# Second SwiGLU: down's pair 1 of k-tiles by seven products of quarters in place of eight

## The chip, the cores and the metric

The kernel runs on one core of a Trainium2 chip. The metric is the device time of one execution, in microseconds (us): the median of several runs, each the time of the slowest core, which here is the only one. Beside the timed runs stands one execution taken by the hardware profiler; its instructions, waits and transfers are what this document calls the profile and the trace. TensorE is called PE, VectorE DVE, ScalarE ACT, GpSimd POOL; SP is the sync engine, which issues most DMAs.

## The reference

Two layers of a transformer trunk on 256 tokens of width 1024, all in fp32. Each layer has a SwiGLU, a mixer (attention) and a second SwiGLU, with an RMSNorm ahead of each:

```python
def rms_norm(x, g):
    xf = x.astype(jnp.float32)
    y = xf * lax.rsqrt(jnp.mean(xf * xf, axis=-1, keepdims=True) + EPS)
    return (y * g.astype(jnp.float32)).astype(x.dtype)

def swiglu(h, w_gate, w_up, w_down):
    return (jax.nn.silu(h @ w_gate) * (h @ w_up)) @ w_down

...
    for layer in range(DEPTH):
        h = rms_norm(x, ffn1_norm[layer])
        x = x + 0.5 * swiglu(h, ffn1_w_gate[layer], ffn1_w_up[layer], ffn1_w_down[layer])
...
        h = rms_norm(x, ffn2_norm[layer])
        x = x + 0.5 * swiglu(h, ffn2_w_gate[layer], ffn2_w_up[layer], ffn2_w_down[layer])
    return rms_norm(x, final_norm)
```

`w_gate` and `w_up` are 1024 x 2816, `w_down` is 2816 x 1024. The change concerns the second of the four SwiGLUs (layer 0, `ffn2`), which the code calls stage 2.

## The kernel before

**Tiles.** The 256 tokens are two token tiles (`tt` 0 and 1) of 128. Every fp32 matrix product is made of parts: a weight tile is split on the core into a high part (`hi`, ACT, line 477) and a low part (`lo`, the rest, DVE, line 480), the activations likewise, and `mm` issues three matmuls for what the document calls one **product**: high by high (line 469), activation high by weight low (470), activation low by weight high (471), each 128x128 by 128x512, into one PSUM bank.

**A SwiGLU.** `ffn` goes through five chunks of 512 columns of gate and up and one of 256; each chunk's gated result (`glu`) goes through `turned_over` (two ACT copies, lines 554 and 558, with a transposing DMA of SP between them, line 556) and `split_psum` (`g_h`, `g_l`), and stays as the left operand of down. Down's 22 k-tiles are taken in 11 pairs, in the order of the table `DOWN`. A pair written `p` is plain: its two weight rows are two splits of 128x1024, and 2 k-tiles x 2 token tiles x 2 column halves make eight products.

**Seven for eight.** A pair written `s` treats the pair's activations (2 token tiles x 2 k-tiles) and weights (2 k-tiles x 2 halves) as two matrices of 2 x 2 blocks and forms the product of these with seven products (`seven`), by sums on both sides, in the manner of Strassen and Winograd. The weight sums are made by `strassen`: after the first split (one block, `b11`) DVE runs three adds (line 395), and the splits that follow are the raw second row of blocks, the two sums in `two`, and the two sums written back over the raw tile:

```python
        splits = [
            Split(second[:, 0:1, :], [1], then=all_sums),
            Split(first, [1]),
            Split(first, [1], kind="sum"),
            Split(second, [1], True, kind="sum"),
        ]
```

The high and low parts of the sums are called `shi` and `slo`; there are three buffers for them, and seven for the plain parts (`FIT`). The activation sums are made when the chunk that holds the pair comes back transposed: `quarters` copies blocks to a tile of that name (ACT, lines 699 and 702) and subtracts (DVE, line 705), `sums_of` runs two more DVE instructions (712, 713) and splits the result into `k..h` (ACT) and `k..l` (DVE). In that case token tile 1 needs one `g_h` and `g_l` block less (384 columns for 512). In the end `combine` adds the four products that are not accumulated in place to x, once for all `s` pairs of the stage. The first `s` pair of a stage also sets the pace at which weights are prepared (`DOWN_RATE`).

The table `SEVEN` does the same with the last k-tiles of some chunks of gate and up: in stage 2 the chunks 1 (three groups of seven products) and 3 (two groups).

**What sets the order.** The order on every engine is the order in which the code issues, with no scheduler behind it. `mm` calls `tick` once per product; `tick` steps the small tasks (silu, glu, transposes, `quarters`), each of which says for how many products it rests, and calls `supply` at a set rate, which issues the next `hi` on ACT and, at the next step, its `lo` on DVE. The raw weights come over SP's queue into three buffers of 1 MB; a new load is issued when the last split of a buffer has been read. An engine works strictly in its order, so an instruction that waits holds up all behind it.

Of the kernel before, what the change touches and what calls it, by code (L numbers as in the profile page):

```python
# [34 lines left out]

DOWN = {
    0: "p0 p1 p2 s3 p4 s5 p6 s7 p8 p10 p9",
    2: "p0 p2 p1 p3 s5 p4 s7 p10 s8 p6 p9",
    3: "p0 p2 s5 s3 p4 s8 p10 p1 s6 p9 p7",
    5: "p3 p0 s2 s5 p4 s1 p9 s7 s8 p6 p10",  # L40
}
# [1525 lines left out]
```

## Time and profile before

| | before |
|---|---|
| timed runs | 944.22 us median of 3 (943.14 to 944.48) |
| profiled execution | 943.06 us, of which the span of instructions is 941.3 us |
| PE busy | 920.8 us (98%) |
| DVE busy | 789.1 us (84%) |
| ACT busy | 679.4 us (72%) |
| mean granted clock of TensorE | 0.998 |

The second SwiGLU begins before 290 us with the plain chunk 0; chunk 1's seven-product groups end near 321 us, down runs from 396 us to about 450 us. Its busy time in some stretches, from the view by windows (busy us with the number of instructions, then the granted clock, the DMA share and GB/s):

```profile
300.00:310.00 10.00, 10.00 (x46) 8.29 (x45) 8.93 (x13) 8.90 (x12) 0.00 (x0) 1.00 0.60 159
310.00:320.00 10.00, 8.01 (x35) 6.13 (x34) 9.93 (x12) 7.74 (x10) 0.00 (x0) 1.00 0.31 105
320.00:330.00 10.00, 10.00 (x45) 8.26 (x44) 8.99 (x11) 6.02 (x7) 0.00 (x0) 1.00 0.89 315
...
400.00:410.00 10.00, 10.00 (x46) 8.29 (x45) 8.17 (x13) 9.17 (x15) 0.00 (x0) 1.00 0.85 270
410.00:420.00 10.00, 10.00 (x45) 8.28 (x45) 9.93 (x13) 6.41 (x9) 0.00 (x0) 1.00 0.54 182
```

The columns after the window are PE, weight loads, DVE, ACT and POOL. A stretch in which PE has 10.00 of 10 is bound by the matmuls; in the one from 310 us PE lacks 2 us while DVE has no pause.

### The profile page before, as it was taken

The page shows a single profiled execution, that of the slowest core. Times are in us where ns is not written, and L with a number is a line of the kernel's source. Part 1 is how long each engine was busy: PE and PEld are TensorE (multiplying, and loading weights), DVE is VectorE, ACT ScalarE, POOL GpSimd, SP SyncE. Part 2 cuts the span into 40 slices and gives each one's busy share as a digit, 9 for nine tenths or more (in the row PEclk, how much of TensorE's full clock was granted, in tenths as well). Part 3 has the DMA queues.
Part 4 walks back from the last instruction along what each step waited for, and adds up shares of the span by engine and source line. Part 5 has one row for each costly group of instructions (what it writes and reads, how often), then busy time and mean ns, then how long its engine had stood idle before and what let it go on. Part 6 is the DMA issues. An engine that isn't in the chain of part 4 may idle for free.

```text
span 941.3 us, 12409 instructions
## 1 busy us (share of the span) xinstructions
PE 920.8 (98%) x4399; PEld 752.5 (80%) x4399; DVE 789.1 (84%) x1228; ACT 679.4 (72%) x1091; POOL 92.6 (10%) x152
## 2 busy tenths in 40 slices
PE   9999999999999999999999999999999999999997
PEld 6887888877778788888888778777878788878886
DVE  6799779778869989788878888999877787988797
ACT  7777875477787777875757778657877577769753
POOL 1300000064410000000100000008030000000001
PEclk9999999999999999999999999999999999999999
DMA  8858865554336677867457777566433458488651
GB/s 297 291 158 255 249 209 216 180 154 99 105 94 199 221 214 235 255 204 265 140 163 236 186 239 223 204 249 172 151 119 135 135 172 253 127 274 254 184 224 45
DMA packets 129343, 183.16 MB, mean 195 GB/s; under 512 B 50688, under 2 KB 63744, under 8 KB 129280
## 3 DMA queue, kind: packets, MB, share of 16 engines
q1 hardware_dynamic: 128704, 181.58, 61.0%
q8 instruction: 34, 0.56, 0.2%
q10 hardware_dynamic: 576, 0.79, 0.2%
q14 instruction: 29, 0.24, 0.1%
HBM read 169.76 MB, written 1.05 MB: 181 GB/s over the span
## 4 chain that ended last, share of the span: by engine, by line
PE 69%; DVE 15%; ACT 7%; DMA 4%; issue 4%; POOL 1%; SPq 0%; POOLq 0%; ACTq 0%; DVEq 0%
PE pj L469 10%; PE pj L470 10%; PE pj L471 9%; PE s L470 9%; PE s L471 9%; PE s L469 9%; DVE lo L480 6%; ACT hi L477 2%; PE o L1039 2%; PE o L470 1%; PE o L471 1%; PE o L469 1%; PE tp L1118 1%; DVE raw L395 1%; DVE two L395 1%
## 5 line engine op out<-in xcount | busy, mean ns | idle before, releaser
L480 DVE TENSOR_TENSOR lo<-raw,hi 128x1024 fp32r<-128x1024 f32 (+1 forms) x372 | 375.9, 1030 | 79.0 <-ACT hi L477 77.2
L477 ACT ACTIVATE hi<-raw 128x1024 fp32r<-128x1024 f32 (+1 forms) x372 | 319.7, 890 | 54.9 <-PE pj L471 14.5
L470 PE MATMUL s<-lo,th 128*128 128x512 f32 x373 | 145.6, 390 | 2.6 <-DVE lo L480 2.6
L469 PE MATMUL pj<-hi,th 128*128 128x512 f32 x367 | 146.6, 400 | 1.3 <-ACT glu L765 1.3
L469 PE MATMUL s<-hi,th 128*128 128x512 f32 x373 | 146.2, 392 | 0.3 <-ACT hi L477 0.3
L471 PE MATMUL s<-hi,tl 128*128 128x512 f32 x373 | 145.3, 390 | 0.0
L470 PE MATMUL pj<-lo,th 128*128 128x512 f32 x367 | 143.5, 391 | 1.7 <-DVE lo L480 1.6
L471 PE MATMUL pj<-hi,tl 128*128 128x512 f32 x367 | 143.2, 390 | 0.0
L470 PEld LDWEIGHTS s<-lo,th 128*128 128x128 f32 x373 | 70.0, 188 | 18.3 <-DVE lo L480 4.2
L469 PEld LDWEIGHTS s<-hi,th 128*128 128x128 f32 x373 | 70.0, 188 | 14.9 <-ACT hi L477 0.6
L470 PEld LDWEIGHTS pj<-lo,th 128*128 128x128 f32 x367 | 69.1, 188 | 16.0 <-DVE lo L480 3.3
L471 PEld LDWEIGHTS s<-hi,tl 128*128 128x128 f32 x373 | 70.0, 188 | 14.4
L469 PEld LDWEIGHTS pj<-hi,th 128*128 128x128 f32 x367 | 69.0, 188 | 15.6 <-ACT glu L765 1.7
L471 PEld LDWEIGHTS pj<-hi,tl 128*128 128x128 f32 x367 | 68.9, 188 | 14.5
L489 POOL TENSOR_TENSOR rstd<-var,mhalf 128x1 f32<-128x1 f32 (+2 forms) x16 | 17.1, 1070 | 594.8 <-DVE var L487 453.4
L558 ACT COPY turned<-glu 128x1024 uint16<-128x1024 uint16 (+1 forms) x48 | 60.1, 1253 | 6.8 <-DMA glu<-turned 6.8
L554 ACT COPY turned<-glu 128x1024 uint16<-128x1024 uint16 (+1 forms) x48 | 46.3, 965 | 14.8 <-DVE glu L792 7.0
L469 PE MATMUL s<-hi,g_h 128*128 128x512 f32 (+1 forms) x131 | 51.4, 392 | 0.0
L471 PE MATMUL s<-hi,g_l 128*128 128x512 f32 (+1 forms) x131 | 50.9, 388 | 0.0
L470 PE MATMUL s<-lo,g_h 128*128 128x512 f32 (+1 forms) x131 | 50.8, 388 | 0.0
L477 ACT ACTIVATE shi<-two 128x1024 fp32r<-128x1024 f32 x30 | 31.7, 1058 | 26.1 <-DVE two L395 25.9
L477 ACT ACTIVATE shi<-raw 128x1024 fp32r<-128x1024 f32 x30 | 31.7, 1056 | 23.5 <-PE s L471 13.0
(483 smaller groups left out, 1681.4 us busy)
## 6 DMA issues: line engine op xcount, KB each, us to landing
raw<-in_ffn_w_down SPq DMA_DIRECT2D x44, 1024.0 KB, 5.2
raw<-in_ffn_w_up SPq DMA_DIRECT2D x28, 1024.0 KB, 5.2
raw<-in_ffn_w_gate SPq DMA_DIRECT2D x26, 1024.0 KB, 5.2
raw<-in_ffn_w_gate SPq DMA_DIRECT2D x35, 512.0 KB, 3.9
raw<-in_ffn_w_up SPq DMA_DIRECT2D x32, 512.0 KB, 5.0
raw<-in_odd_w_qkv SPq DMA_DIRECT2D x12, 1024.0 KB, 5.4
raw<-in_even_w_in SPq DMA_DIRECT2D x4, 1024.0 KB, 5.0
raw<-in_even_w_out SPq DMA_DIRECT2D x8, 512.0 KB, 5.7
```

The costliest lines, as they stand in the source:

```text
L395: add = lambda o, x, y: self.nc.vector.tensor_tensor(o, x, y, op=ALU.add)
L469: mm(ps, h, wh, start=first, stop=False)
L470: mm(ps, h, wl, start=False, stop=False)
L471: mm(ps, l, wh, start=False, stop=last)
L477: self.nc.scalar.activation(hi, src, AF.Copy)
L480: self.nc.vector.tensor_tensor(lo, src, hi.bitcast(F32), op=ALU.subtract)
L489: nc.gpsimd.tensor_tensor(r[:, :n], v[:, :n], self.mhalf[:, :n], op=ALU.pow)
L554: self.nc.scalar.copy(planes.rearrange("p (h c) -> p h c", h=2), back.rearrange("p (c h) -> p h c", h=2))
L558: self.nc.scalar.copy(planes.rearrange("p (c h) -> p h c", h=2), back.rearrange("p (h c) -> p h c", h=2))
L1039: self.nc.tensor.matmul(O[64 * s : 64 * s + 64, i * P : i * P + P], v(b0 + i, s, kc), pT[s][:, i, kc, :], start=(kc == 0), stop=(kc == 1),)
L1118: nc.tensor.transpose(tb[:, o : o + P], p[:, i, kc * P : kc * P + P], self.ident)
```

## The change

One entry of the table of down's pairs: in stage 2, pair 1 (k-tiles 2 and 3, the second pair of down's 22 k-tiles) is `s` instead of `p`. It stays the third pair in the order, and is now the first `s` pair of the stage, so that the tasks that `seven` finishes on its first call, the banks it takes and `DOWN_RATE` come two pairs earlier.

```diff
 DOWN = {
     0: "p0 p1 p2 s3 p4 s5 p6 s7 p8 p10 p9",
-    2: "p0 p2 p1 p3 s5 p4 s7 p10 s8 p6 p9",
+    2: "p0 p2 s1 p3 s5 p4 s7 p10 s8 p6 p9",
     3: "p0 p2 s5 s3 p4 s8 p10 p1 s6 p9 p7",
     5: "p3 p0 s2 s5 p4 s1 p9 s7 s8 p6 p10",
 }
```

Pair 1's activations lie in chunk 0, which comes back transposed while chunk 1 runs. On DVE, in the second and third group of chunk 1, the rows before are these (`turned_3198` is chunk 0's result for token tile 1; `raw_3100` and `raw_3132` are the weights of the second and third group):

```order
L480 TENSOR_TENSOR slo_3252<-two_3229,shi_3251 128x1024
L480 TENSOR_TENSOR g_0_l_3279<-turned_3198,g_0_h_3278 128x512
L480 TENSOR_TENSOR slo_3286<-raw_3100,shi_3285 128x1024
L480 TENSOR_TENSOR lo_3295<-raw_3132,hi_3294 128x512
L395 TENSOR_TENSOR two_3301<-raw_3132 128x1024
L395 TENSOR_TENSOR raw_3132<-two_3301,raw_3132 128x512
L395 TENSOR_TENSOR raw_3132<-raw_3132 128x512
L480 TENSOR_TENSOR lo_3306<-raw_3132,hi_3305 128x1024
```

And now, from the same `slo` on:

```order
L480 TENSOR_TENSOR slo_3254<-two_3229,shi_3253 128x1024
L705 TENSOR_TENSOR quarters_3237<-turned_3198,quarters_3237 128x2x128
L480 TENSOR_TENSOR slo_3289<-raw_3100,shi_3288 128x1024
L480 TENSOR_TENSOR g_0_l_3286<-turned_3198,g_0_h_3285 128x384
L712 TENSOR_TENSOR quarters_3237<-quarters_3237 128x128
L713 TENSOR_TENSOR quarters_3237<-quarters_3237 128x128
L480 TENSOR_TENSOR lo_3301<-raw_3132,hi_3300 128x512
L395 TENSOR_TENSOR two_3307<-raw_3132 128x1024
L395 TENSOR_TENSOR raw_3132<-two_3307,raw_3132 128x512
L395 TENSOR_TENSOR raw_3132<-raw_3132 128x512
L480 TENSOR_TENSOR lo_3312<-raw_3132,hi_3311 128x1024
```

Three instructions are new, and the `g_l` is smaller and stands behind the second `slo`. The last row is the `lo` that PE's first product with the third group's raw row needs. Further on, one `k2l` is new, between the first and the second `lo` of chunk 2.

On ACT, at the same place, before (`turned_3182` is token tile 0):

```order
L558 COPY turned_3182<-glu_3151 128x2x512
L477 ACTIVATE g_0_h_3237<-turned_3182 128x512
L477 ACTIVATE hi_3240<-raw_3100 128x1024
L477 ACTIVATE shi_3251<-two_3229 128x1024
L558 COPY turned_3198<-glu_3192 128x2x512
L477 ACTIVATE g_0_h_3278<-turned_3198 128x512
L477 ACTIVATE shi_3285<-raw_3100 128x1024
```

and now:

```order
L558 COPY turned_3182<-glu_3151 128x2x512
L699 ACTIVATE quarters_3237<-turned_3182 128x256
L477 ACTIVATE g_0_h_3239<-turned_3182 128x512
L477 ACTIVATE hi_3242<-raw_3100 128x1024
L477 ACTIVATE shi_3253<-two_3229 128x1024
L558 COPY turned_3198<-glu_3192 128x2x512
L702 ACTIVATE quarters_3237<-turned_3198 128x128
L477 ACTIVATE g_0_h_3285<-turned_3198 128x384
L477 ACTIVATE shi_3288<-raw_3100 128x1024
```

Two copies are new, both ahead of the `shi` of the second group's last sums. A `k2h` follows later, between the two `shi` of the third group.

The third place is DVE in the first pairs of down. Before (`raw_3853` is pair 2, `raw_3908` pair 1, `raw_3937` pair 3):

```order
L480 TENSOR_TENSOR lo_4000<-raw_3853,hi_3999 128x1024
L480 TENSOR_TENSOR lo_4012<-raw_3908,hi_4011 128x1024
L480 TENSOR_TENSOR lo_4025<-raw_3908,hi_4024 128x1024
L480 TENSOR_TENSOR k14l_4019<-quarters_3914,k14h_4018 128x512
L480 TENSOR_TENSOR lo_4042<-raw_3937,hi_4041 128x1024
```

and now, with pair 2 called `raw_3863`, pair 1 `raw_3918` and pair 3 `raw_3947`:

```order
L480 TENSOR_TENSOR lo_4010<-raw_3863,hi_4009 128x1024
L480 TENSOR_TENSOR lo_4022<-raw_3918,hi_4021 128x512
L395 TENSOR_TENSOR two_4028<-raw_3918 128x1024
L395 TENSOR_TENSOR raw_3918<-two_4028,raw_3918 128x512
L395 TENSOR_TENSOR raw_3918<-raw_3918 128x512
L480 TENSOR_TENSOR lo_4039<-raw_3918,hi_4038 128x1024
L480 TENSOR_TENSOR k14l_4033<-quarters_3924,k14h_4032 128x512
L675 SCALAR_TENSOR_TENSOR glu_4067<-s_3999,rstd_3030,silu_4053 128x256
L480 TENSOR_TENSOR slo_4070<-two_4028,shi_4069 128x1024
L480 TENSOR_TENSOR g_16_l_4064<-turned_3949,g_16_h_4063 128x512
L480 TENSOR_TENSOR slo_4084<-raw_3918,shi_4083 128x1024
L480 TENSOR_TENSOR lo_4101<-raw_3947,hi_4100 128x1024
```

Two splits of pair 1 have become four with three adds between them, and pair 3's first `lo` stands behind all of them. From pair 7's weights on DVE and ACT have the same order as before.

## The prediction

> **What bounds the kernel now.** I read the page first, for the shares and for the chain of work that ended last.
>
> ```profile
> span 941.3 us, 12409 instructions
> PE 920.8 (98%) x4399; PEld 752.5 (80%) x4399; DVE 789.1 (84%) x1228; ACT 679.4 (72%) x1091; POOL 92.6 (10%) x152
> PE 69%; DVE 15%; ACT 7%; DMA 4%; issue 4%; POOL 1%; SPq 0%; POOLq 0%; ACTq 0%; DVEq 0%
> ```
>
> PE is busy 98% of the span and carries 69% of the chain; DVE carries 15%. So fewer matmuls shorten the kernel only where PE is not itself waiting, and more work on DVE lengthens it only where PE is waiting for DVE. Which of the two holds differs from place to place, so the next view is the table of waits, for PE, over the second SwiGLU alone (290 to 500 us reaches past its end on both sides). Its columns are the total in us, the number of times and the longest.
>
> ```profile
> PE s L470 <- DVE lo L480: 2.0, 1, 2.0
> ```
>
> There is one wait in 210 us, and it is 2.0 us long. The PE timeline shows where it is, and also what a product costs (start, duration, line and operands).
>
> ```profile
> 315.03 0.39 PE L469 MATMUL s<-hi,th 128*128 128x512 f32 x1
> 317.41 0.50 PE L470 MATMUL s<-lo,th 128*128 128x512 f32 x1 [1.99 <-DVE lo L480]
> ...
> 407.33 0.39 PE L469 MATMUL o<-hi,g_h 128*128 128x512 f32 x1
> ...
> 412.77 0.39 PE L469 MATMUL o<-hi,g_h 128*128 128x512 f32 x1
> ```
>
> The wait stands in chunk 1 of the gates, in the last of its three groups of seven products: PE has multiplied with the high part and waits for the low part of the same weights. The other two rows are the first matmul of down's pair 1 and the first of the pair after it: 24 matmuls, eight products of three, in 5.44 us. One matmul takes 0.227 us from start to start (the 0.39 us durations overlap), and **one product takes 0.68 us**.
>
> What DVE does ahead of the wait shows whether it has slack there. These are all its rows from 310.07 on (the "..." stands for the two adds that follow the one shown at 313.55).
>
> ```profile
> 310.07 1.22 DVE L480 TENSOR_TENSOR slo<-two,shi 128x1024 fp32r<-128x1024 f32 x1
> 311.21 0.68 DVE L480 TENSOR_TENSOR g_l<-turned,g_h 128x512 fp32r<-128x512 f32 x1
> 311.81 1.22 DVE L480 TENSOR_TENSOR slo<-raw,shi 128x1024 fp32r<-128x1024 f32 x1
> 312.95 0.68 DVE L480 TENSOR_TENSOR lo<-raw,hi 128x512 fp32r<-128x512 f32 x1
> 313.55 1.22 DVE L395 TENSOR_TENSOR two<-raw 128x1024 f32<-128x1024 f32 x1
> ...
> 316.14 1.22 DVE L480 TENSOR_TENSOR lo<-raw,hi 128x1024 fp32r<-128x1024 f32 x1
> ```
>
> No row has an idle time in brackets: DVE works without a pause up to the lo at 316.14, which ends at 317.36, and PE goes on at 317.41. **Here DVE is the bound, and whatever is put ahead of 316.14 on DVE is added to the stall.** From start to start an slo or lo of 1024 columns costs 1.14 us (311.81 to 312.95), a lo of 512 columns 0.60, a g_l of 512 columns 0.60, and the three adds together 2.59 (313.55 to 316.14).
>
> **What the change removes.** Pair 1 of down takes seven products instead of eight: three matmuls, 0.68 us, at a place (407 to 413 us) where PE waits for nothing. That is a gain of **0.68 us**, if the weights stay ahead of PE there.
>
> **What it adds in chunk 1.** The four blocks of pair 1's activations are in the first chunk of the gates, whose transposed halves come back just ahead of the stall. By the orders shown above, L705, L712 and L713 now stand on DVE between 311.21 and 312.95, and L699 and L702 on ACT ahead of the slo's high part. Their price is read where chunk 3 does the same for pair 7. DVE first, then ACT.
>
> ```profile
> 392.76 0.41 DVE L705 TENSOR_TENSOR quarters<-turned,quarters 128x256 f32<-128x256 f32 x1
> 393.10 0.55 DVE L480 TENSOR_TENSOR g_l<-turned,g_h 128x384 fp32r<-128x384 f32 x1
> 393.56 0.28 DVE L712 TENSOR_TENSOR quarters<-quarters 128x128 f32<-128x128 f32 x1
> 393.88 0.29 DVE L713 TENSOR_TENSOR quarters<-quarters 128x128 f32<-128x128 f32 x1
> ```
>
> ```profile
> 386.17 0.42 ACT L699 ACTIVATE quarters<-turned 128x256 f32<-128x256 f32 x1
> 386.49 0.62 ACT L477 ACTIVATE g_h<-turned 128x512 fp32r<-128x512 f32 x1
> ...
> 392.19 0.31 ACT L702 ACTIVATE quarters<-turned 128x128 f32<-128x128 f32 x1
> 392.41 0.51 ACT L477 ACTIVATE g_h<-turned 128x384 fp32r<-128x384 f32 x1
> 392.88 1.05 ACT L554 COPY turned<-glu 128x1024 uint16<-128x1024 uint16 x1
> ```
>
> From start to start: L705 0.34, g_l of 384 columns 0.46, L712 0.32, L713 at most 0.29; on ACT L699 0.32, L702 0.22, g_h of 384 columns 0.47. ACT's own rows at the stall show what is pushed.
>
> ```profile
> 306.12 0.63 ACT L477 ACTIVATE g_h<-turned 128x512 fp32r<-128x512 f32 x1
> ...
> 309.94 0.63 ACT L477 ACTIVATE g_h<-turned 128x512 fp32r<-128x512 f32 x1
> 310.48 1.04 ACT L477 ACTIVATE shi<-raw 128x1024 fp32r<-128x1024 f32 x1
> ```
>
> ACT has no pause from 306.12 to 310.48 either. L699 goes in at 306.12 (+0.32), L702 at 309.94 (+0.22), and the second g_h shrinks from 0.54 to 0.47 (-0.07). So shi starts 0.47 later, at 310.95, and ends at 311.99. On DVE the g_l at 311.21 gives way to L705, which ends the slot at 311.55; the slo then waits for shi until about 311.99, 0.44 us of new idle time. It takes 1.14 (313.13), g_l 0.46 (313.59), L712 0.32 (313.91), L713 0.29 (314.20). The lo of 512 columns starts at **314.20 instead of 312.95**, and the three adds and the lo behind it move by the same 1.25 us. The stall grows by **1.25 us**, from 1.99 to 3.24.
>
> Bounds: if the wait for shi were covered, the stall grows by 0.81. PE's earlier products of the group (it takes the slo of 311.81 at 313.1) get late by 0.2 to 0.3 us, but that is time that PE would otherwise spend in the stall. Behind the stall come k2h on ACT and k2l on DVE. k2l stands between the first two lo of chunk 2, and PE takes the third of these at 324.34 (DVE, then PE):
>
> ```profile
> 319.54 2.35 DVE L480 TENSOR_TENSOR lo<-raw,hi 128x1024 fp32r<-128x1024 f32 x2
> ...
> 322.42 2.35 DVE L480 TENSOR_TENSOR lo<-raw,hi 128x1024 fp32r<-128x1024 f32 x2
> ```
>
> ```profile
> 324.34 0.39 PE L470 MATMUL pj<-lo,th 128*128 128x512 f32 x1
> ```
>
> The third lo ends at 322.42 + 1.22 = 323.64, 0.70 us ahead of its matmul, and the shift by the stall is the same for both. k2l, a 128x512 subtraction like the lo at 312.95, takes 0.60 of that; 0.1 us is left. I cost it at nothing; if that cover fails, it adds up to 0.60, and k2h on ACT up to 0.5 more (its g_h neighbour of 512 columns took 0.54).
>
> **What it adds in down.** Pair 1's weights need 0.60 + 2.59 + 3 x 1.14 on DVE for 2 x 1.14 before: **+4.33 us** of DVE ahead of the pairs that follow, and PE comes to those 0.68 us earlier. The tightest of them is pair 5's last sum; its slo on DVE, the lo ahead of down, and the product that reads it on PE:
>
> ```profile
> 395.28 3.64 DVE L480 TENSOR_TENSOR lo<-raw,hi 128x1024 fp32r<-128x1024 f32 x3 [0.46 <-ACT hi L477]
> ...
> 412.07 1.22 DVE L480 TENSOR_TENSOR slo<-raw,shi 128x1024 fp32r<-128x1024 f32 x1
> ...
> 422.91 1.23 DVE L480 TENSOR_TENSOR slo<-raw,shi 128x1024 fp32r<-128x1024 f32 x1 [0.61 <-ACT shi L477]
> ```
>
> ```profile
> 421.84 0.39 PE L470 MATMUL s<-slo,g_h 128*128 128x512 f32 x1
> ```
>
> It is ready at 413.29 for 421.84: 8.55 us, less 4.33 and 0.68 leaves **3.5 us**. For pair 1 itself the new order puts eight instructions (0.60 + 2.59 + 1.14 + 0.60 + about 0.4 + 1.14 + 0.60 + 1.14) behind the lo that ends its slot at 396.42, so the last sum is ready near 404.7; PE reads it at 407.33 + 5 x 0.68 + 0.23 = 410.96, 6 us later. At 422.91 DVE begins to wait for buffers that PE frees, and there the lag is worked off. So in down I cost all of it at nothing; the cover is those 3.5 us.
>
> Queues: pair 1's raw weights are held until that last slo, 404.7 instead of 398.9, and SP now issues the load of pair 4 behind it, between the two transposing DMAs of the 256-column chunk, where before it stood ahead of both. The second of these waits behind the load now; what it carries is read in pair 10, two pairs after pair 4. The DMA view and ACT's timeline give the load and its first reader:
>
> ```profile
> raw<-in_ffn_w_down SPq DMA_DIRECT2D x10, 1024.0 KB, 5.4
> ```
>
> ```profile
> 410.82 1.99 ACT L477 ACTIVATE hi<-raw 128x1024 fp32r<-128x1024 f32 x2
> ```
>
> 404.7 + 5.4 = 410.1 is still ahead of 410.82, and ACT is itself some 3 us later by then. POOL's order is unchanged.
>
> **The sum.** -0.68 + 1.25 = **+0.57 us**. The profiled execution took 943.06 us (941.3 of span and 1.8 around it), so 943.6 on its scale. It was the fastest of those shown; the median of the timed runs is 944.22, and there the sum gives **944.8 us**, 0.06% more.
>
> [...] The stall would be the longest pause of PE inside the kernel. [...] No run so far shows a pause of that length.
>
> **Rivals.**
> 1. The growth of the stall is covered in part. For it: 0.44 of it is a wait for ACT that a small shift of ACT's order would remove, and L705, L712 and L713 may overlap more than their rows. Without that wait the sum is -0.68 + 0.81 = +0.1 (944.3); were all of it covered, -0.68 (943.5). Against: neither DVE nor ACT has a pause in the 6 us ahead. 20%.
> 2. Down runs short of weights (the slower side). The place is pair 5's last sum or pair 4's load; it decides when the lag on DVE is 8.5 us instead of the 5.0 worked out, for instance when a load takes over 3 us longer than 5.4. The price is a stall of the size of the one that DVE makes now, 2.0: +0.57 + 2.0 = +2.6, **946.8 us**. Against: 3.5 us of cover. 7%.
> 3. The pause lets the clock drop. The nearest row is the start of the program, where six matmuls of 512 columns on zeros run before PE is warm:
>
> ```profile
> 1.45 2.74 PE L1488 MATMUL o<-zeros 128*128 128x512 bf16 x6 [1.45 <-DVE zeros L1482]
> ```
>
>    They take (2.74 - 0.39) / 5, at most 0.47 us each for 0.227 later; six of them lose 1.4 us. +0.57 + 1.4 = +2.0, 946.2 us. Against: the stall of 1.99 us is followed by matmuls 0.23 apart. 4%.
> 4. k2l and k2h uncover a second stall in chunk 2: +0.57 + 0.60 + 0.5 = +1.7, 945.9 us at most. 9%.
>
> That the change doesn't do what it says is excluded by the order: three matmuls fewer on PE, the seven of pair 1 in their place.
>
> **How the numbers follow.** The forecast holds 60%, the rivals 20, 7, 4 and 9. About 0.2%, 1.9 us, is what a measurement of this kernel can tell from no change. The forecast, rival 1 and rival 4 lie inside it; rival 2 and most of rival 3 are slower by more, 9% with the scatter of the runs (943.14 to 944.48); nothing here gains 1.9 us, and 3% is left for what I have not seen. The range goes from rival 1's full cover less some scatter, 943.2, to rival 4 and the edge of rival 3, 946.2.
>
> **What would show it.** Right: PE's wait near 317 us at 3.0 to 3.4 us with a lo on DVE as its end, shi and slo near 311 and 312 us, no wait of PE between 395 and 450 us, and pair 1 done in 4.76 us. The stall near 2.8 means rival 1; a wait of PE on lo or slo after 410 us rival 2; matmuls over 0.4 us apart after the stall rival 3; a wait near 325 us rival 4. The prediction is wrong if the stall doesn't grow, or if PE's gaps elsewhere, far behind, change.

## The result, and the profile after

The kernel after takes 950.77 us (median of 6 runs, 949.98 to 954.40), the kernel before beside it 943.51 (943.14 to 944.48): the ratio is 1.0077, 95% interval 1.0066 to 1.0088. The change makes the kernel slower by 0.8%. Forecast were 944.8 us and a range of 943.2 to 946.2; the loss is more than ten times the sum that was worked out (+0.57). The profiled execution took 950.39 us, 7.33 more than that of before.

The same lines of the page of after: span, busy time, and the chain's shares.

```profile
span 948.6 us, 12416 instructions
PE 924.1 (97%) x4396; PEld 754.1 (79%) x4396; DVE 794.7 (84%) x1237; ACT 681.5 (72%) x1096; POOL 92.5 (10%) x152
PE 61%; DVE 19%; ACT 10%; DMA 4%; issue 4%; POOL 0%; SPq 0%; POOLq 0%; ACTq 0%; DVEq 0%
```

PE has three matmuls fewer and is busy for 3.3 us longer: matmuls have become slower somewhere. DVE's 5.6 us more are the added work. DVE and ACT took 7 points of the chain from PE, so new waits exist. PE's table of waits for the second SwiGLU (290 to 500 us; total, times, longest) shows two where before there was one:

```profile
PE tp L525 <- DVE x L612: 3.2, 1, 3.2
PE s L470 <- DVE lo L480: 2.8, 1, 2.8
```

**The first place, chunk 1.** PE's timeline of after around the old pause:

```profile
315.48 0.40 PE L469 MATMUL s<-hi,th 128*128 128x512 f32 x1
318.63 0.50 PE L470 MATMUL s<-lo,th 128*128 128x512 f32 x1 [2.76 <-DVE lo L480]
...
319.46 0.63 PE L470 MATMUL s<-lo,g_h 128*128 128x512 f32 x1
319.89 0.63 PE L471 MATMUL s<-hi,g_l 128*128 128x512 f32 x1
...
322.86 0.39 PE L469 MATMUL s<-shi,th 128*128 128x512 f32 x1
```

PE goes on at 318.63 in place of 317.41, 1.22 us later. Behind it, from 319.46 to 322.86, matmuls start 0.43 us apart and not 0.23. From 318.63 to 322.86 it takes 4.23 us for what took 2.62 before: 1.61 us lost without a wait. The windows view, cut at the times at which the clock changes, gives PE's busy time, then the other engines' and, behind POOL, the granted clock:

```profile
316.01:319.42 3.41, 0.79 (x3) 0.67 (x4) 3.36 (x4) 3.33 (x4) 0.00 (x0) 1.00 0.47 183
319.42:322.83 3.41, 3.41 (x9) 2.67 (x8) 3.41 (x5) 3.41 (x5) 0.00 (x0) 0.50 0.22 39
322.83:326.24 3.41, 3.41 (x16) 2.82 (x15) 3.41 (x4) 0.90 (x3) 0.00 (x0) 1.00 1.01 362
```

The granted clock is 0.50 for 3.41 us, from 319.42 to 322.83, and 1.00 on both sides.

**The second place, behind down.** PE's timeline of after, where the next stage's first transposes stand:

```profile
452.10 0.39 PE L471 MATMUL s<-hi,g_l 128*128 128x512 f32 x1
455.68 0.90 PE L525 MATMUL tp<-mats,x 128*128 128x128 f32 x4 [3.19 <-DVE x L612]
...
456.81 0.63 PE L470 MATMUL s<-lo,g_h 128*128 128x512 f32 x1
```

PE waits 3.19 us for x, the output of the SwiGLU's first half, and then the granted clock is 0.50 again, from 455.95 to 459.37. In the kernel before, this place has no wait (PE, then DVE):

```profile
450.18 0.60 PE L525 MATMUL tp<-mats,x 128*128 128x128 f32 x4
```

```profile
444.47 0.68 DVE L938 SCALAR_TENSOR_TENSOR x<-pj,x 128x512 f32<-128x512 f32 x1
...
447.72 0.68 DVE L612 SCALAR_TENSOR_TENSOR x<-o,x 128x512 f32<-128x512 f32 x1
```

x is ready at 448.40 for 450.18: 1.8 us of cover. In the kernel after the same rows of DVE read:

```profile
441.08 4.62 DVE L480 TENSOR_TENSOR lo<-raw,hi 128x1024 fp32r<-128x1024 f32 x4
447.43 2.36 DVE L480 TENSOR_TENSOR lo<-raw,hi 128x1024 fp32r<-128x1024 f32 x2 [1.72 <-ACT hi L477]
450.55 1.23 DVE L480 TENSOR_TENSOR lo<-raw,hi 128x1024 fp32r<-128x1024 f32 x1 [0.76 <-ACT hi L477]
451.70 0.68 DVE L938 SCALAR_TENSOR_TENSOR x<-pj,x 128x512 f32<-128x512 f32 x1
...
454.94 0.68 DVE L612 SCALAR_TENSOR_TENSOR x<-o,x 128x512 f32<-128x512 f32 x1
```

x comes 7.22 us later than before while PE comes 2.15 later (452.33 for 450.18): 5.07, less 1.8 of cover, is the wait. The three lo ahead of the combine (L938 to L952) belong to the next stage's gates. They have two waits of their own, since ACT, which makes the high parts ahead of them, waits for the gates' weights (and 1.11 us more at 449.46):

```profile
446.34 2.01 ACT L477 ACTIVATE hi<-raw 128x1024 fp32r<-128x1024 f32 x2 [3.60 <-DMA raw<-in_ffn_w_gate]
```

SP issues these loads from 441.19 on, in before from 434.41 on, since down frees the buffers later.

The sum of after: restart of PE behind the first wait +1.22, half clock +1.61, pair 1's product -0.68 (its 21 matmuls run from 410.17 to 414.93, 4.76 us), x late +3.35 (by starts: 455.68 against 450.18, less 2.15), half clock +1.62 (from this L525 to the one eight transposes on, 455.68 to 463.71, 8.03 us for 6.41). Together +7.1 of the 7.33.

### The profile page after: what moved, and what is told of

Same layout as the page of the kernel before. It is cut to its first block, busy times and chain, and to the rows that moved or that the text cites. A ratio compares the mean times of both kernels' runs of the same rounds, so it can differ in the third digit from the quotient of the medians.

```text
span 948.6 us, 12416 instructions
## 1 busy us (share of the span) xinstructions
PE 924.1 (97%) x4396; PEld 754.1 (79%) x4396; DVE 794.7 (84%) x1237; ACT 681.5 (72%) x1096; POOL 92.5 (10%) x152
## 4 chain that ended last, share of the span: by engine, by line
PE 61%; DVE 19%; ACT 10%; DMA 4%; issue 4%; POOL 0%; SPq 0%; POOLq 0%; ACTq 0%; DVEq 0%
PE pj L469 9%; DVE lo L480 9%; PE pj L470 8%; PE pj L471 8%; PE s L470 8%; PE s L471 8%; PE s L469 8%; ACT hi L477 3%; DMA glu<-turned 2%; DVE raw L395 2%; ACT turned L558 2%; DVE two L395 2%; PE o L1039 2%; PE tp L1118 1%; DVE slo L480 1%
## 5 line engine op out<-in xcount | busy, mean ns | idle before, releaser
L480 DVE TENSOR_TENSOR slo<-raw,shi 128x1024 fp32r<-128x1024 f32 x31 | 37.8, 1220 | 12.8 <-ACT shi L477 12.8
```

The lines of the kernel that those rows point to most:

```text
L480: self.nc.vector.tensor_tensor(lo, src, hi.bitcast(F32), op=ALU.subtract)
```

## The experiments

All sizes below are PE's time from the first transposes ahead of the second SwiGLU (272.85 us in before) to the L525 at 456.59, 183.74 us in the profile of before; I call it the stretch. Other runs of before, in c3 and c4, give 183.76 and 183.79, so 0.1 us can be told there. The time of a whole run can't do that: on the chips of the experiments the kernel before itself spread from 943.3 to 948 or 950 us. Three single runs of over 1100 us, two of before and one of b3, are left out of the ratios.

| run | stretch, against before | profiled execution | median | ratio to before, 95% interval |
|---|---|---|---|---|
| after | +7.18 | 950.39 | 950.77 | 1.0077 (1.0066 to 1.0088) |
| e1 sums alone | +3.16 | 947.44 | 947.51 | 1.0039 (1.0020 to 1.0058) |
| e2 two quarters | +3.71 | 950.28 | 948.02 | 1.0038 (1.0023 to 1.0053) |
| e3 late | +6.47 | 950.17 | 949.24 | 1.0055 (1.0039 to 1.0071) |
| e4 hold | +2.15 | 945.32 | 945.44 | 1.0001 (0.9988 to 1.0014) |
| b1 before, hold | +0.02 | 944.30 | 943.53 | 0.9979 (0.9966 to 0.9992) |
| b2 hold, late | -0.57 | 942.47 | 943.17 | 0.9975 (0.9964 to 0.9987) |
| b3 hold, filled pause | +0.45 | 945.94 | 946.46 | 1.0003 (0.9991 to 1.0015) |
| b4 hold, late, two | -0.29 | 943.26 | 943.15 | 0.9971 (0.9957 to 0.9985) |
| c1 hold, both late | -0.01 | 943.91 | 943.82 | 0.9986 (0.9975 to 0.9997) |
| c2 before, hold, both late | -0.06 | 943.70 | 943.56 | 0.9983 (0.9972 to 0.9994) |

**e1: the activation sums without the seven products.** Against before:

```diff
-        paired = {2 * pair: [] for kind, pair in down if kind == "strassen"}
+        paired = {2 * pair: [] for kind, pair in down if kind == "strassen" or (self.now.n, pair) == (2, 1)}
```

(The last g_l of chunk 0 stays 512 columns wide, as pair 1 still multiplies with it.)

> The kernel before, with one part of the change alone: the four blocks of pair 1's activations are also added up in chunk 0 of the gates (L699, L702, L705, L712, L713 and the two k2), but pair 1 keeps its eight products, so no DVE work is added in down. Two-places theory (the sums cost a longer pause at 317 us and a halved clock behind it; the other half of the loss is made in down and paid at L525): the wait of PE at 317 us is 3.2 to 3.4 us long in place of 2.0, some nine matmuls behind it stand 0.43 us apart, PE does not wait at L525, and the profiled execution takes 943.1 + 1.3 + 1.6 = 946.0 us. Rival (the clock has another cause than the pause, for instance the kernel as a whole): the wait grows the same, matmuls stay 0.23 us apart, 944.4 us. Second rival (the wait at L525 comes from the shift at 317 us and not from down): L525 waits here too and the time is near 950.

Measured: its waits of PE from 300 to 460 us are

```profile
PE s L470 <- DVE lo L480: 2.8, 1, 2.8
PE s L470 <- DVE slo L480: 0.3, 1, 0.3
```

The pause is 2.75 us (3.2 to 3.4 were expected; PE also gets to it later), the half clock stands behind it (matmuls 0.43 us apart from 320.17 on), and there is no wait at L525. The stretch is 3.16 longer: 1.3 + 1.6 expected, and 0.3 more, the second wait. The profiled execution, 947.44 us, is 1.4 above the 946.0 expected; a second half clock, from 545.34 on (the mean granted clock from 543.26 to 546.67 is 0.81), lies behind the stretch. So the sums in chunk 0 make the first place by themselves, and the second place needs the added work in down.

**e2: two buffers for the quarters.** Against after, in L698:

```diff
-                paired[f] = self.t([P, 4, P], "quarters")
+                paired[f] = self.t([P, 4, P], "quarters", 2 if self.now.n == 2 else 1)
```

It aims at this row of ACT in the kernel after, with a wait that before does not have there:

```profile
404.34 0.42 ACT L699 ACTIVATE quarters<-turned 128x256 f32<-128x256 f32 x1 [2.52 <-DVE k14l L480]
```

The next pair's quarters wait for the last reader of the only buffer, k14l, which DVE now does later, behind pair 1's weights.

> The kernel after, with two buffers for the quarters in the second SwiGLU, so that L699 in chunk 3 no longer has to wait for pair 1's k14l. Theory A (the one buffer carries the lag from DVE to ACT and back, and without that the lag is the 4.3 us of added work less cover): the 2.5 us wait of ACT at 404 us is gone, the wait of PE at L525 shrinks from 3.2 to at most 1 us, the half clock behind it is gone too, and the profile takes 945.5 to 947.5 us. Theory B (DVE's added 4.33 us alone make the lag): the wait at 404 us is gone, but that at L525 stays at 2.5 to 3.2 us and the time stays within 1 us of 950.4. In both the wait at 317 us stays 2.76 us with the half clock behind it.

Measured: ACT's row starts at 401.86 without a wait, and PE's wait at L525 is halved.

```profile
PE tp L525 <- DVE x L612: 1.5, 1, 1.5
```

The result lies between the theories: the single buffer is worth 1.7 of the 3.2 us, and with it the half clock goes (the granted clock is 1.00 from 450.19 to 460.42); the rest stays with DVE's added work, and e4 below shows what its place in line has to do with it. The stretch is +3.71. The profiled execution is still 950.28, because 3.3 us were lost far behind, most of them at the L525 of the stage after (a wait of 2.48 us at 637.95, with a half clock). c3, the kernel before unchanged, has a wait of 2.18 us with a half clock at the same place, so such a loss comes without the change too.

**e3: the half of the sums behind the pause.** Against after; the second token tile of chunk 0 is turned 12 products later:

```diff
-    def turned_over(self, m, w):
+    def turned_over(self, m, w, late=0):
...
-        yield TURN_WAIT[1]
+        yield TURN_WAIT[1] + late
...
-            tb = yield from self.turned_over(m, w)
+            tb = yield from self.turned_over(m, w, 12 if (self.now.n, tt, f0) == (2, 1, 0) else 0)
```

> The kernel after, with the transposed half of chunk 0's second token tile taken 12 products later, so that L558, L702, L705, both splits of g, L712, L713 and k2 stand behind the wait at 317 us on DVE and ACT. Theory (the pause sets the clock): the wait at 317 us is at most 1.5 us, the matmuls behind it stay 0.23 us apart, and PE gains 1.3 + 1.6 = 2.9 us there; of this the wait at L525 takes some back, since PE gets there earlier while DVE's lag in down stays, so 947.5 to 949 us. Rival (the half clock is not from the pause): matmuls 0.43 us apart at 318 to 323 us as in the kernel after, 949 to 950 us.

Measured:

```profile
PE tp L525 <- DVE x L612: 4.1, 1, 4.1
PE s L470 <- DVE lo L480: 1.5, 1, 1.5
```

```profile
450.19:453.60 3.41, 0.09 (x1) 0.00 (x0) 3.34 (x6) 0.00 (x0) 0.00 (x0) 1.00 0.71 263
453.60:457.01 3.41, 2.59 (x8) 2.24 (x9) 3.41 (x7) 1.44 (x5) 0.00 (x0) 0.50 0.03 11
457.01:460.42 3.41, 3.41 (x9) 2.53 (x8) 1.55 (x5) 2.04 (x5) 0.00 (x0) 0.50 0.00 0
```

The first place behaves as expected, with the granted clock at 1.00 behind a pause of 1.54 (317.98 to 321.39). But nearly all of it is paid back at L525: a longer wait, and behind it a granted clock of 0.50 for 6.82 us in place of 3.41. The time came out above the range expected. What PE gains ahead of a late x, it waits for at x.

**e4: the combine ahead of the next gates' weights.** Against after; `room()` lets no split of the next gates through until the combine has been put in line:

```diff
-        if not self.whole:
+        if not self.whole or self.hold and getattr(self.whole[0], "gate", False):
             return False
...
+            for split in self.whole[-len(views):]: split.gate = nk == 4
...
-        order = [i for i, (kind, _) in enumerate(down) if kind == "strassen"]
+        order, self.hold = [i for i, (kind, _) in enumerate(down) if kind == "strassen"], self.now.n == 2
...
-                    self.rate, self.due = ENDS[self.now.n]
+                    (self.rate, self.due), self.hold = ENDS[self.now.n], False
```

> The kernel after, with the next stage's gate weights not split before the second SwiGLU's combine has been put in line, so that L612's x does not stand on DVE behind lo's that wait for late loads. Theory (the wait at L525 is made by that place in line): the wait at L525 falls from 3.2 us to below 1, the half clock behind it goes, and the profile takes 945.5 to 947 us, unless the gates' first products then wait for their weights. Rival (x is late because the whole lag of DVE is on it): the wait at L525 stays above 2 us, time 949 to 951.

Measured (DVE; one line was added, so L938 is L939 here, and L612 is L613):

```profile
441.31 4.63 DVE L481 TENSOR_TENSOR lo<-raw,hi 128x1024 fp32r<-128x1024 f32 x4
445.85 0.68 DVE L939 SCALAR_TENSOR_TENSOR x<-pj,x 128x512 f32<-128x512 f32 x1
...
450.24 0.68 DVE L613 SCALAR_TENSOR_TENSOR x<-o,x 128x512 f32<-128x512 f32 x1
```

x comes 4.7 us earlier than in after, though the four lo ahead come no earlier (441.31): what made x late was its place in line. PE doesn't wait there, the granted clock is 1.00 from 450.19 to 460.42, and the stretch is +2.15, which is 1.22 + 1.61 - 0.68, the first place alone. So the second place cost 5.0 of the 7.2 us. (The profiled execution, 945.32, lies just under the range expected.)

**b1: the control for e4.** The kernel before with e4's edit.

> The kernel before with the hold of e4 alone (the next stage's gate weights are not split ahead of the second SwiGLU's combine). A control: PE of the kernel before does not wait at L525, so if the hold only repairs what the change broke, this kernel gains nothing: 943.1 us in the profile, within 0.5. If the hold is a gain of its own (or a cost, with PE waiting for the gates' first weights behind the SwiGLU), it shows here as a shift of more than 0.5 us, and e4's gain on the kernel after has to be read less that.

Measured: the stretch is 183.76 us, +0.02. The hold repairs what the change broke and gains nothing there by itself. The profiled execution missed the 943.1 expected: it took 944.30, but 0.9 of these 1.2 us lie ahead of the stretch and the rest far behind it. Its timed runs lay 0.2% under those of before (0.9979, 0.9966 to 0.9992); its profile shows no place for that, and the cause stays open.

**b3: the pause filled, for the clock.** e4, with eight matmuls between the two on either side of the pause, and a tile of zeros for them at the start of the program:

```diff
-        mm(ps, h, wh, start=first, stop=False)
+        mm(ps, h, wh, start=first, stop=False); self.fill = 0 * len([mm(ps[:32, :], self.z32, wh, start=False, stop=False) for _ in range(self.fill)])
...
+                self.fill = 8 * (self.now.n == 2 and f0 == 4 and name == "00" and last)
...
-        warm(WARM)
+        warm(WARM); self.z32 = one.tile([P, 32], F32R, tag="z32", name="z32"); nc.scalar.activation(self.z32, zeros[:, :32], AF.Copy)
```

> e4 with eight matmuls on a tile of zeros (32 columns of weights, 512 moving columns, added to the open sum, which they leave as it is) set between the last product's first matmul and the one that waits at 317 us: 8 x 0.227 = 1.8 us of work inside the pause of 2.76. Nothing else differs from e4, and PE resumes at the same moment. If the pause itself halves the clock by the idle share of the window that ends behind it (e4: 22% busy in that window): the share rises to over 60%, the matmuls behind stay 0.23 us apart, and the time falls by 1.6 us to 943.7. If the clock falls for another reason (a fixed place, the load on the chip): the half clock stays and the time is 945.3.

Measured:

```profile
317.16 0.39 PE L469 MATMUL s<-hi,th 128*128 128x512 f32 x1
317.38 2.02 PE L469 MATMUL s<-hi,z 128*32 128x512 f32 x8
320.32 0.51 PE L470 MATMUL s<-lo,th 128*128 128x512 f32 x1 [0.91 <-DVE lo L480]
...
321.13 0.40 PE L470 MATMUL s<-lo,g_h 128*128 128x512 f32 x1
```

The matmuls behind stand 0.23 us apart (the next is at 321.37), and the stretch falls from +2.15 to +0.45, by 1.70 for 1.6 expected: from the restart to the twelfth matmul on it takes 2.66 us for e4's 4.17, 1.51 less, and the rest is a pause that ends a little earlier. From 317.98 to 321.39 the mean granted clock is 1.00, for e4's 0.61: between these two runs the half clock went when PE's idle time was filled. The whole time, 945.94, missed its 943.7: 2.1 us lie ahead of the stretch, where the tile of zeros is made, which the expectation had not counted.

**b2 and b4: the edits of e3 and e4 together, and those of e2, e3 and e4.**

> The kernel after with both e3 and e4: the half of the sums behind the wait at 317 us, and combine ahead of the next gates' splits. If the two losses are independent and nothing else is lost: e4's 945.3 less the shorter pause (2.76 - 1.54 = 1.22) and the half clock (1.6): 942.5 us, 0.6 under the kernel before, which is pair 1's 0.68. Rival: PE now gets to L525 2.8 us earlier while e4's x had 1.6 us of cover and DVE follows by only some 2, so a wait of 0 to 1 us appears at L525: 942.5 to 943.5.

> e2, e3 and e4 together: the hold, the late half of the sums, and two buffers for the quarters. If b2 has a rest of the wait at L525, this one takes it away, since e2 brought DVE forward by 2 us: 942.5 us. If b2 has no such rest, the second buffer changes nothing: the same as b2 within 0.3 us.

Measured: b2's stretch is -0.57 and its profile 942.47, as the first case has it; the pause is 1.53, and L525 does not wait. b4's stretch is 0.28 longer than b2's and its profile 0.8: the second buffer gains nothing more, and PE has a new wait of 0.29 us for a lo at 368.61. So the loss in chunk 1 can be won back once x is no longer late; alone, e3 won back 0.7 us. The seven products are worth what was forecast: counted from the start of the stretch, PE comes to pair 1's first product 0.11 us later in b2 than in before, and pair 1 takes 4.76 us for 5.44. Against before b2's ratio is 0.9975 (0.9964 to 0.9987), but b1, without the change, has 0.9979: the change's own share of 0.6 us is below what timed runs can tell.

**c1 and c2: the pause made shorter still.** The kernels after (c1) and before (c2), with e4's hold and, in e3's last line,

```diff
-            tb = yield from self.turned_over(m, w)
+            tb = yield from self.turned_over(m, w, 24 if (self.now.n, f0) == (2, 0) else 0)
```

> b2 with both token tiles of chunk 0 turned 24 products later, so that the first g_l (0.60 us on DVE) leaves the rows ahead of the wait at 317 us too. The pause there goes from 1.53 to 0.9 us and the profile to 942.5 - 0.6 = 941.9 us; if the rows that now come behind the pause are late for PE near 325 us, up to 0.5 of it is lost: 941.9 to 942.4.

> The control for c1: the kernel before (eight products in pair 1) with the same hold and the same 24 products. Two g_l of 0.60 leave the rows ahead of the pause: 1.99 - 1.2 = 0.8 us, so the profile takes 943.1 - 1.2 = 941.9 us. Theory (pair 1's seven products are worth their 0.68 us once the sums and the hold are out of the way, but the shift of the g_l is a gain of its own): c1 is faster than c2 by 0.4 to 0.7 us. Rival (the whole gain of b2 and c1 is that of the shift): c1 and c2 within 0.2 us.

Measured: the pause at 317 us is 0.94 in both, as expected, and nothing is gained in either. PE in c1:

```profile
317.17 0.50 PE L470 MATMUL s<-lo,th 128*128 128x512 f32 x1 [0.94 <-DVE lo L480]
337.50 0.50 PE L470 MATMUL s<-lo,th 128*128 128x512 f32 x1 [0.99 <-DVE lo L480]
369.58 0.50 PE L470 MATMUL pj<-lo,th 128*128 128x512 f32 x1 [0.51 <-DVE lo L480]
```

The work that was moved out of the pause comes back as waits of PE for DVE at 337 and 369 us; here the pause was moved, not removed. That DVE alone is the bound from chunk 1 to chunk 3 is not shown: in c1 it has waits of its own there for ACT's hi, one of them of 2.42 us. Both expected times were missed, by 1.5 to 2 us, and c1 was not faster than c2, as the rival had it. But the seven products do not lose their worth: c1 comes to pair 1's first product 0.67 us later than before does and c2 0.06 earlier (both counted from the start of the stretch), and pair 1 gives c1 the 0.68 back. What is lost ahead of pair 1 when its activation sums are put in there, 0.1 us in b2, 0.4 in b4 and 0.7 in c1, decides whether anything is left.

**c3 and c4: the kernel before, for the clock.**

> The kernel before, unchanged, for its clock. [...]

> [...]

Measured: 946.64 and 944.42 us, pauses at 317 us of 1.96 and 1.99, full clock behind both; the mean granted clock of the whole span is 0.997 and 0.999. So the kernel before kept the clock behind this pause in all three of its profiles. b2 lost the clock behind two pauses of 0.76 and 1.29 us, each shorter than the pause of 1.99 that kept it:

```profile
314.57:317.98 3.41, 1.88 (x9) 1.25 (x8) 3.38 (x5) 3.00 (x4) 0.00 (x0) 1.00 0.70 270
...
539.85:543.26 3.41, 1.51 (x6) 0.96 (x6) 2.83 (x3) 3.38 (x6) 0.00 (x0) 1.00 0.46 121
543.26:546.67 3.41, 3.41 (x8) 2.65 (x9) 2.58 (x4) 3.30 (x5) 0.00 (x0) 0.50 1.05 401
```

In the profile of before the same two pauses, 0.76 us up to 541.06 and 1.27 up to 543.76, have the clock at 1.00 from 537.99 to 548.23. So in these runs the length of a pause alone does not tell whether the clock falls behind it; what does is not shown. b2's half clock cost it nothing in the end: it lost 1.5 us against before there and had them back by 597 us, since before has waits for DVE on the way (559.70, 594.16 and 597.37) that b2 has not. Of c3's extra 2.2 us against c4, 1.5 lie behind the L525 of the stage after, with a half clock as in e2, and 0.8 at the transposes of L547 some 28 us later.

## Why the prediction was wrong

- **Step "a product is 0.68 us": right.** Pair 1 took 4.76 us, as forecast.
- **Step "the stall grows by 1.25 us": right in the time of the restart, wrong in the length of the stall.** After shows:

```profile
311.16 0.42 DVE L705 TENSOR_TENSOR quarters<-turned,quarters 128x256 f32<-128x256 f32 x1
312.04 1.22 DVE L480 TENSOR_TENSOR slo<-raw,shi 128x1024 fp32r<-128x1024 f32 x1 [0.46 <-ACT shi L477]
...
314.17 0.68 DVE L480 TENSOR_TENSOR lo<-raw,hi 128x512 fp32r<-128x512 f32 x1
...
317.36 1.22 DVE L480 TENSOR_TENSOR lo<-raw,hi 128x1024 fp32r<-128x1024 f32 x1
```

  The new wait for shi is 0.46 (0.44 forecast), the lo at 314.17, the restart +1.22. The pause itself reads 2.76 and not 3.24, since PE came to it 0.45 later (315.48 for 315.03); the prediction had 0.2 to 0.3 of this lateness, and did not take it off the stall. By the sign set down for it (a stall near 2.8 means rival 1), this would have been misread: the sign should have been the time of the restart.
- **Step on the clock (the sum has no loss for it): failed,** 1.61 us here and 1.62 at L525. The pause was shorter than forecast (2.76 us for 3.24), and the clock fell all the same. It was rival 3, at 4%, with a price of 1.4 that was nearly right. PE was not idle all through ahead of it: after's granted clock was 0.50 behind 3.41 us with 0.79 us of work, b2's behind 3.41 us with 1.51; in b3, with the pause filled, it was 1.00.
- **Step on k2: the outcome is right, the 0.1 us of cover was not put to the test.** Nothing waits near 325 us, but PE comes there 1.6 us later than forecast, for the half clock.
- **Step on pair 1's weights and load: the outcome is right (PE waits nowhere between 395 and 450 us), the times are not.** The last slo was to be ready near 404.7; after has

```profile
408.36 1.22 DVE L480 TENSOR_TENSOR slo<-raw,shi 128x1024 fp32r<-128x1024 f32 x1
```

  which ends 4.9 us later, at 409.58, and the load behind it starts at 409.61. Down began 2.8 us late on DVE (the lo of 395.28 stands at 398.09), which is the shift from chunk 1 with its half clock; the other 2.1 us are those that e2 gives back.
- **Step "at 422.91 DVE begins to wait for buffers that PE frees, and there the lag is worked off. So in down I cost all of it at nothing": failed, and it is the larger error,** 3.35 us and the second half clock. The cover was looked up at the tightest product inside down (3.5 us) and held there. The next reader behind down, x for L525 with 1.8 us of cover, was not looked at, and the lag of DVE had not been worked off. Before shows how little idle time there was for it:

```profile
433.15 1.23 DVE L480 TENSOR_TENSOR slo<-raw,shi 128x1024 fp32r<-128x1024 f32 x1 [1.29 <-ACT shi L477]
434.30 4.62 DVE L480 TENSOR_TENSOR lo<-raw,hi 128x1024 fp32r<-128x1024 f32 x4
```

  From 422.91 to the four lo DVE has two waits, 0.61 and 1.29 us, 1.9 together, for a lag that the prediction put at 5.0. In after both are gone, DVE has no pause from 413.21 to 445.70, and the four lo come at 441.08, 6.8 us late, of which 2.15 are PE's own. Two things that the walk of down left out are shown by the runs: the one quarters buffer, which let ACT and DVE wait for each other (e2: 1.7 us of the wait), and the combine's place behind the next gates' lo, whose weights arrive late when down frees its buffers late (e4: without it the wait is gone).
- Rival 2 (a stall behind the lag of DVE, 2.0 us) had the kind of the second loss, but the wrong place: it was to stand on a lo or slo in down.

## What to carry to other kernels

When a lag on an off-bound engine is costed at nothing, follow it to the last thing that this engine does for the bound engine in the stage and in the one behind, not only to the tightest row inside; a lag ends only where that engine has idle time of its own, so add this idle time up (here 1.9 us for a lag of 5.0), and a single buffer can eat it. What stands in line on that engine may be more than what is needed: moving the result ahead of the next stage's preparation gave back 5.0 of 7.2 us. A pause of PE can cost more than its length: after's granted clock was 0.50 for 3.41 us behind pauses of 2.76 and 3.19 us, which cost 1.61 and 1.62 us more, and b2's behind two pauses of 0.76 and 1.29 us, which cost 1.5 (b2 got them back later, where before waits anyway). Behind the pause of 1.99 us in before the clock was 1.00: work that put off the end of this pause by 1.22 us cost 2.83.

## What was not expected of the hardware

In the middle of the kernel after the granted clock falls to 0.50, twice, for 3.41 us each; in the profile of before it falls only behind PE's last work (from 937.35 us on). A matmul of 512 columns then takes 0.43 us from start to start in place of 0.23. What PE did ahead of the fall, by the windows view:

| run | stretch (3.41 us) | PE busy, us | granted clock in the 3.41 us behind |
|---|---|---|---|
| after | 316.01 to 319.42 | 0.79 | 0.50 |
| after | 452.54 to 455.95 | 0.27 | 0.50 |
| b2 | 539.85 to 543.26 | 1.51 | 0.50 |
| e3 | 450.19 to 453.60 | 0.09 | 0.50 |
| e3 | 453.60 to 457.01 (itself at 0.50) | 2.59 | 0.50 |
| b2 | 314.57 to 317.98 | 1.88 | 1.00 |
| before | 312.71 to 316.13 | 2.71 | 1.00 |
| before | 316.13 to 319.54 | 2.13 | 1.00 |

The busy times are modelled, and these are single profiles; more than these values is not shown.

The same kernel can scatter by such a step: c3 and c4 are both the kernel before, and of their waits of 2.18 and 1.99 us at the L525 of the stage after, the first lost the clock and 1.5 us, the second did not (mean granted clock of the span 0.997 and 0.999). How much of the spread of the kernel before on the experiments' chips this is, was not tried.
